# SBUF slots on multiples of 2048 bytes, and a convolution without pad columns, in a hybrid decoder layer

## Chip, cores, metric

One core of a Trainium2 chip runs the whole layer in one launch. The metric is the device time of that launch in microseconds, the median of several runs.

## What is computed

One decoder layer on T = 512 tokens with D = 1024, float32 in and out. The reference, cut to its frame:

```python
def hybrid_layer(x, ...):
    h = rms_norm(x, norm1_g)
    z = h @ w_in + b_in
    (mq, mk, mv, mo, mi, mf, fq, fk, fv, ff, rx, ry, gq, gk, gv, gg, ga, gates) = split_cols(z)
    y_ml = sigmoid(mo) * rms_norm(mlstm(mq, mk, mv, mi, mf))         # 4 heads of 128
    y_fx = forgetting_attention(fq, fk, fv, ff)                       # 4 heads of 128
    y_lru = rg_lru_branch(rx, ry, ...)     # causal conv of width 4, gates, scan, times gelu(ry)
    y_gla = silu(gg) * rms_norm(gla(gq, gk, gv, log_alpha))
    yb = einsum("bsnw,nwd->bsnd", stack([y_ml, y_fx, y_lru, y_gla]), w_branch)
    x = x + (sum over branches of sigmoid(gates) * yb) @ w_o
    h2 = rms_norm(x, norm2_g)
    return x + square(relu(h2 @ w_up)) @ w_down                       # D_FF = 4096
```

The convolution takes `y[t] = cb + cw3 x[t] + cw2 x[t-1] + cw1 x[t-2] + cw0 x[t-3]` in each channel, with x zero before the first token.

## The kernel before

**The large products.** Every product with a weight matrix is made from exact halves: a value is split into `hi` and `lo`, and hi·hi + hi·lo + lo·hi are summed in PSUM. One such product of a 128-row k-tile and 512 columns is three matmuls of 128x128 stationary and 512 moving columns, written by `Group.unit`. A group is one of two kinds. In an fm group (L266 to L268) the stationary operand is a piece of the weights (`whi`, `whi`, `wlo`) and the moving one is 512 columns of activations (`hh`, `hl`, `hh`). In a tm group (L270 to L272) the stationary operand is 128 columns of the activations (`hh`, `hh`, `hl`) and the moving one is 512 columns of the weights (`whi`, `wlo`, `whi`). There are 864 triples of the first kind and 480 of the second, 4032 matmuls. A stretch of 48 of them (4 k-tiles, 4 banks, 3 matmuls) uses one 1 MB chunk of weights; it is called a stage here.

**Weights.** 83 chunks of 1 MB come through SP's queue into `wraw` (2 buffers); ACT casts each half chunk to `whi` (L201) and DVE subtracts to get `wlo` (L202).

**Slots.** Activations live in 16 pieces of SBUF, called slots. `Slots.get` hands out the slot that has been free longest, `free` puts one back at the end. A tile's name tells both: `s7_54` is slot 7, handed out by the 54th call. A slot has 2064 float32 columns per partition, 8256 bytes, which is 32·256 + 64. In the built program the slots stand one behind the other and the weight pieces behind them; 16·8256 is 516·256. So slot i begins 64·i bytes behind slot 0 modulo 256, and `whi` and `wlo` have the residue of slot 0. The text calls the residue of a stationary piece's address minus that of a moving one, modulo 256, the **offset** of a pair; every smaller step inside a slot (512 columns, 128 columns) is a multiple of 256 bytes. With slot i against a weight piece the offset is 64·i modulo 256 where the slot is stationary, and 256 minus that where it moves: it is 0 for s0, s4, s8 and s12 alone.

**The branches.** `gens` and `pump` put pieces of the four branches (mLSTM, forgetting attention, RG-LRU, GLA) between the triples of the large products; Tile's scheduler sets each engine's final order from the program as written. `prep(n)` makes the exact halves `yhi[n]` (ACT, L442) and `ylo[n]` (DVE, L443) of a branch's result, which the projection of that branch then multiplies with `w_branch`. The convolution of the RG-LRU (L664 to L666) runs on DVE over `rx`, which holds 4 groups of 515 columns, 3 of them zero (memsets at L1141), and writes `xc`. Then come the gate products (L675, evacuated by ACT at L676 and by DVE at L677), exponentials and tanh on ACT (L686, L687), and products on DVE (L699, L700). The sigmoid of a merge gate is ACT's L883. Around the output projection, the gains of the second norm (L1171) and x are loaded again into slots, and L931 and L933 read them.

**Order.** PE, ACT, DVE and POOL each run their instructions in the order the scheduler wrote; an instruction whose data or slot is not free holds everything behind it on its engine.

Of the kernel before, what the change touches and what calls it, by code (L numbers as in the profile page):

```python
# [24 lines left out]
H = 4  # L25
# [9 lines left out]
PINC, PINK, PINN, PINS, LAG = 7, 7, 3, 4, 2  # L35
SLOT = 2064
NSLOT = 16


class Slots:  # L40
    """Eight-kilobyte pieces of SBUF, handed out and taken back in the order of emission."""

    def __init__(self, pool):
        self.pool = pool
        self.free_ids = deque(range(NSLOT))
        self.owner = {}
        self.n = 0

    def get(self, dtype=F32):
        i = self.free_ids.popleft()  # L50
        self.n += 1
        t = self.pool.tile([P, SLOT], dtype, tag=f"slot{i}", name=f"s{i}_{self.n}")
        self.owner[id(t)] = (i, t)
        return t

    def free(self, *ts):
        for t in ts:
            i, _ = self.owner.pop(id(t))
            self.free_ids.append(i)


@with_exitstack
def tile_hybrid(ctx, tc, x, norm1_g, w_in, b_in, ml_norm_g, fx_qnorm_g, fx_knorm_g, lru_conv_w,
# [38 lines left out]

    # ---------------------------------------------------------------- loads and constants
    xs = [slots.get(), slots.get()]
# [21 lines left out]
    def vector_loads():  # L126
        """Every per-channel vector as rows of 128; one transpose turns the rows into columns."""
        r = 0
# [42 lines left out]
    nc.gpsimd.memset(nhalf, -0.5)  # L171
    # selecting mask: 1 where t >= s, for [s, t]
    msel = ctile([P, P], name="msel")
    nc.gpsimd.memset(msel, 1.0)
    nc.gpsimd.affine_select(msel, msel, pattern=[[1, P]], compare_op=ALU.is_ge, fill=0.0, base=0, channel_multiplier=-1)

    # ---------------------------------------------------------------- weight stream
    # Chunks of four k-tiles by 512 columns come in whole; the exact halves hi + lo are made in pieces of two k-tiles.
    jobs, pieces = [], []
# [43 lines left out]
    def pinned(ins):  # L223
        """Keeps an instruction behind what its engine was given before it."""
        tc.keep_in_program_order(ins)
        return ins
# [23 lines left out]
    class Group:  # L250
        """One 512-column group of a product: z^T (fm) or z (tm), with a callback per finished bank."""

# [21 lines left out]
        def run(self, first=None):  # L274
            """first, where given, does the first chunk."""
            if self.pre:
# [29 lines left out]

    # ---------------------------------------------------------------- first norm, x to feature-major
    hTh = [slots.get(F32R), slots.get(F32R)]
# [8 lines left out]
    def rstd_of(ssum, n, width):  # L317
        """(ssum / n + EPS) ** -0.5 on a [128, width] tile: three Newton steps from a guess of the exponent."""
        v = tiny.tile([P, 16], F32, tag="rsv", name="rsv")[:, :width]
        y = tiny.tile([P, 16], F32, tag="rs", name="rs")[:, :width]  # L320
        t = tiny.tile([P, 16], F32, tag="rst", name="rst")[:, :width]
        nc.vector.tensor_scalar(v, ssum, 1.0 / n, EPS, op0=ALU.mult, op1=ALU.add)
        nc.vector.tensor_scalar(y.bitcast(I32), v.bitcast(I32), 1, None, op0=ALU.arith_shift_right)
        nc.vector.tensor_scalar(y.bitcast(I32), y.bitcast(I32), -1.0, float(0x5F3759DF), op0=ALU.mult, op1=ALU.add)
        for _ in range(3):
            nc.vector.tensor_mul(t, y, y)
            nc.vector.scalar_tensor_tensor(t, t, -0.5, v, op0=ALU.mult, op1=ALU.mult)
            nc.vector.scalar_tensor_tensor(y, t, 1.5, y, op0=ALU.add, op1=ALU.mult)
        return y
# [28 lines left out]

    # ---------------------------------------------------------------- small columns: ga, mi, mf, ff
    small = ctile([P, 512], name="small")  # L360
# [4 lines left out]
    def causal(ap, rows_are_queries, fill):  # L365
        """A diagonal block [128, 128]: fill where the key comes after the query."""
        sgn = 1 if rows_are_queries else -1
# [4 lines left out]
    def small_unit():  # L372
# [21 lines left out]
        yield  # L394
        # log_sigmoid of rows 64.. and its running sum over the tokens
        e = w2()
# [37 lines left out]

    # ---------------------------------------------------------------- forgetting attention
    ybr, yhi, ylo = {}, {}, {}
# [9 lines left out]
    def fox():  # L446
# [30 lines left out]
        def soft(h, tb):  # L477
            """Logits of one block of queries against the keys up to it, and their softmax."""
            n = (tb + 1) * P
# [57 lines left out]

    # ---------------------------------------------------------------- per-head norm of a token-major branch
    def norm_piece(num, tbs, hs, den=None):
        """In place: the heads hs of the blocks tbs of num [128, tb, h, 128], over their root mean square.  # L540

        With den [128, tb, h] num is first divided by it, where only the norm's EPS feels it.
        """
        nh, nt = hs.stop - hs.start, tbs.stop - tbs.start
# [18 lines left out]
    def norm_turn(num, gname, gate, y, h):  # L563
        """Head h feature-major, times its gain and gate."""
        ps = sm()
# [6 lines left out]

    # ---------------------------------------------------------------- mLSTM
    mq, mk, mv, mo = [None], [None], [None], [None]
# [56 lines left out]

    # ---------------------------------------------------------------- RG-LRU
    rx, ry = [None], [None]
    XP = 515

    def lru():
# [4 lines left out]
        lam = vecs[:, vrow["lam"] : vrow["lam"] + 4]  # L641
        # softplus(-lam) = max(-lam, 0) + log1p(exp(-|lam|)), log1p(z) = 2 atanh(z / (2 + z))
        nc.vector.scalar_tensor_tensor(z, lam, -1.0, lam, op0=ALU.mult, op1=ALU.max)
# [17 lines left out]
        for b in range(4):  # L661
            xf = rx[0][:, b * XP : (b + 1) * XP]
            s = slice(b * 512, (b + 1) * 512)
            nc.vector.tensor_scalar(xc[:, s], xf[:, 0:512], col("cw", 0 * 4 + b), col("cb", b), op0=ALU.mult, op1=ALU.add)  # L664
            for j in (1, 2, 3):
                nc.vector.scalar_tensor_tensor(xc[:, s], xf[:, j : j + 512], col("cw", j * 4 + b), xc[:, s], op0=ALU.mult, op1=ALU.add)  # L666
            yield
# [11 lines left out]
        slots.free(xc)  # L679
        # rg = 8 softplus(-lambda) r, a = exp(-rg), 1 - a^2 = tanh(rg) (1 + a^2)  # L680
        a = slots.get()
# [5 lines left out]
        nc.scalar.activation(rg[:, :2048], rg[:, :2048], AF.Tanh)  # L687
        # gelu(y) = 0.5 y (1 + tanh(sqrt(2/pi) (y + 0.044715 y^3)))
        for b in range(4):
# [31 lines left out]

    # ---------------------------------------------------------------- gated linear attention
    gqk, gv, gg = [None], [None], [None]

    def gla():
# [6 lines left out]

        # log_alpha and its sums feature-major: [128 (two heads), tokens], a pair of heads at a time
        las, ts_ = [w2(), w2()], [w2(), w2()]
# [39 lines left out]
        yield from steps(PINK)  # L774
        # k-hat token-major: [128 s, block, pair, 128]
        kh = slots.get()
# [75 lines left out]

    # ---------------------------------------------------------------- the rest of the input projection
    def ev_bias(cell, name, base=0, width=512, off=0):
# [8 lines left out]
    g_mo = fm_group(C_MO, ev_bias(mo, "mo"))  # L863
    g_rx = fm_group(C_RX, ev_bias(rx, "rx", 0, XP, 3))
    g_ry = fm_group(C_RY, ev_bias(ry, "rx", 4))
# [4 lines left out]

    # ---------------------------------------------------------------- merge groups
    merged = [None, None]
# [36 lines left out]

    # ---------------------------------------------------------------- output projection, residual  # L910
    xgh, xgl = [None, None], [None, None]
# [31 lines left out]

    # ---------------------------------------------------------------- channel mixer
    Rh, Rl = [None] * 4, [None] * 4
# [39 lines left out]

    # ---------------------------------------------------------------- order of the weight stream
    plan = [g_fq, g_fk, g_fv, g_gqk, g_gv, g_mq, g_mk, g_gg, g_mv, g_mo, g_rx, g_ry]
# [16 lines left out]

    # first chunk: the norm of each block of tokens, and the exact halves of its transpose, as the blocks come in
    sums, rstd1, pg = {}, {}, []
# [100 lines left out]

    # ---------------------------------------------------------------- run: input projection with the branches between
    g_sm = small_unit()
# [21 lines left out]
    g_gg.run()  # L1131
    mv[0] = slots.get()
    nc.gpsimd.memset(mv[0].rearrange("p (h c) -> p h c", c=129)[:, :, P : P + 1], 1.0)
    g_mv.run()
# [4 lines left out]
    rx[0] = slots.get()  # L1139
    for b in range(4):  # L1140
        nc.gpsimd.memset(rx[0][:, b * XP : b * XP + 3], 0.0)  # L1141
    g_rx.run()
# [72 lines left out]
```

## Time and profile before

| what | us |
|---|---|
| median of 3 runs | 1063.26 |
| lowest and highest run | 1063.24 and 1063.74 |
| span of the profiled execution | 1060.3 |
| PE busy in the span | 1032.8 (97%) |
| DVE, ACT, POOL busy | 489.7, 378.0, 24.4 |
| DMA, mean | 94 GB/s, 99.48 MB |

The profile gives the span of its one execution, from the first to the last instruction, and not that execution's own time; the median of the runs lies 3.0 us above the span. Busy time of PE counts a matmul from its start to its modelled end, so that neighbours overlap: the distance between the starts of two matmuls tells what one costs, and the duration in a row is longer than that. Times in the rows are from the span's start.

### The profile page before, as it was taken

How to read it: one execution, taken by the hardware profiler on the slowest of the kernel's cores; microseconds unless marked ns; L12 is line 12 of the kernel's file. 1: busy time of each engine (PE TensorE's matmuls, PEld its weight loads, DVE VectorE, ACT ScalarE, POOL GpSimd, SP SyncE). 2: the span in 40 equal slices, each digit the busy share in tenths (PEclk: the TensorE clock that was granted, in tenths of full speed). 3: DMA queues.
4: the chain of work that ended last, by engine and by line, in shares of the span. 5: the costliest groups of instructions: out<-in, count | busy, mean ns of one | idle time of the engine just before them, and what ended most of it. 6: DMA issues, size and time to landing. Idle time of an engine off the chain costs nothing.

```text
span 1060.3 us, 11180 instructions
## 1 busy us (share of the span) xinstructions
PE 1032.8 (97%) x4545; PEld 825.7 (78%) x4545; DVE 489.7 (46%) x796; ACT 378.0 (36%) x514; POOL 24.4 (2%) x66
## 2 busy tenths in 40 slices
PE   7996899999998999999999999999999999999998
PEld 5885777777877877888888888888888888888886
DVE  5583265246732887533542345554442324544221
ACT  5240444364352457332322233243431113333110
POOL 2000011000000100000000000000000000000000
PEclk9998899999999999999999999999999999999999
DMA  6569421222395212323323342223232232232321
GB/s 185 179 56 76 128 80 42 78 80 80 47 67 125 80 47 74 119 80 119 120 86 112 120 138 81 80 86 113 80 105 94 80 119 80 87 112 80 111 88 40
DMA packets 54086, 99.48 MB, mean 94 GB/s; under 512 B 7253, under 2 KB 7373, under 8 KB 54034
## 3 DMA queue, kind: packets, MB, share of 16 engines
q1 hardware_dynamic: 51762, 92.74, 32.8%
q10 hardware_dynamic: 1872, 4.72, 1.2%
q0 software_dynamic: 400, 1.31, 0.5%
q8 instruction: 35, 0.57, 0.2%
q14 instruction: 17, 0.14, 0.0%
HBM read 94.56 MB, written 2.10 MB: 91 GB/s over the span
## 4 chain that ended last, share of the span: by engine, by line
PE 91%; DMA 7%; DVE 1%; ACT 0%; SPq 0%; issue 0%; POOL 0%; DVEq 0%; ACTq 0%
PE acc L266 18%; PE acc L268 18%; PE acc L267 18%; PE acc L270 10%; PE acc L272 10%; PE acc L271 10%; DMA wraw<-in_w_in_dram 5%; DMA s<-nrows 2%; PE sm L606 1%; PE sm L481 1%; PE sm L508 1%; PE sm L675 1%; PE sm L592 0%; PE sm L498 0%; PE sm L919 0%; PE sm L467 0%
## 5 line engine op out<-in xcount | busy, mean ns | idle before, releaser
L202 DVE TENSOR_TENSOR wlo<-wraw,whi 128x1024 fp32r<-128x1024 f32 x166 | 202.6, 1223 | 386.3 <-ACT whi L201 385.1
L266 PE MATMUL acc<-s,whi 128*128 128x512 f32 x864 | 349.9, 405 | 14.3 <-DVE s L345 12.5
L268 PE MATMUL acc<-s,wlo 128*128 128x512 f32 x864 | 341.4, 395 | 0.0
L267 PE MATMUL acc<-s,whi 128*128 128x512 f32 x864 | 340.3, 394 | 0.0
L201 ACT CAST whi<-wraw 128x1024 fp32r<-128x1024 f32 x166 | 173.5, 1048 | 400.4 <-PE acc L267 183.6
L266 PEld LDWEIGHTS acc<-s,whi 128*128 128x128 f32 x864 | 163.0, 189 | 54.3 <-DVE s L345 12.7
L270 PE MATMUL acc<-whi,s 128*128 128x512 f32 x480 | 193.8, 404 | 0.2 <-ACT s L1042 0.2
L267 PEld LDWEIGHTS acc<-s,whi 128*128 128x128 f32 x864 | 163.1, 189 | 38.7 <-issue 1.9
L268 PEld LDWEIGHTS acc<-s,wlo 128*128 128x128 f32 x864 | 162.8, 188 | 38.1
L271 PE MATMUL acc<-wlo,s 128*128 128x512 f32 x480 | 190.4, 397 | 0.4 <-DVE wlo L1049 0.3
L272 PE MATMUL acc<-whi,s 128*128 128x512 f32 x480 | 190.5, 397 | 0.0
L270 PEld LDWEIGHTS acc<-whi,s 128*128 128x128 f32 x480 | 91.3, 190 | 21.9 <-ACT s L1042 0.9
L272 PEld LDWEIGHTS acc<-whi,s 128*128 128x128 f32 x480 | 90.7, 189 | 21.9 <-DVE s L1043 1.1
L271 PEld LDWEIGHTS acc<-wlo,s 128*128 128x128 f32 x480 | 90.7, 189 | 21.0 <-DVE wlo L1049 1.0
L883 ACT ACTIVATE s<-acc,vecs 128x512 f32<-128x512 f32 x32 | 22.0, 687 | 43.6 <-PE acc L268 43.6
L958 DVE TENSOR_TENSOR w<-w 128x512 f32<-128x512 f32 x32 | 22.1, 690 | 22.3 <-ACT w L956 22.3
L960 DVE TENSOR_TENSOR s<-w,s 128x512 fp32r<-128x512 f32 x32 | 22.1, 690 | 16.5 <-ACT s L959 16.5
L956 ACT ACTIVATE w<-acc 128x512 f32<-128x512 f32 x32 | 19.1, 598 | 28.7 <-PE acc L268 28.7
L959 ACT CAST s<-w 128x512 fp32r<-128x512 f32 x32 | 19.8, 619 | 25.5 <-DVE w L958 25.5
L856 ACT ACTIVATE s<-acc,vecs 128x512 f32<-128x512 f32 x28 | 18.9, 684 | 25.7 <-PE acc L268 25.6
L971 DVE SCALAR_TENSOR_TENSOR s<-acc,r,s 128x512 f32<-128x512 f32 x16 | 12.0, 749 | 31.5 <-PE acc L272 31.5
L896 DVE TENSOR_TENSOR w<-acc,s 128x512 f32<-128x512 f32 x24 | 16.4, 685 | 0.6
(212 smaller groups left out, 584.4 us busy)
## 6 DMA issues: line engine op xcount, KB each, us to landing
wraw<-in_w_in_dram SPq DMA_DIRECT2D x39, 1024.0 KB
wraw<-in_w_up_dram SPq DMA_DIRECT2D x16, 1024.0 KB
wraw<-in_w_down_dram SPq DMA_DIRECT2D x16, 1024.0 KB
wraw<-in_w_branch_dram SPq DMA_DIRECT2D x8, 1024.0 KB
wraw<-in_w_o_dram SPq DMA_DIRECT2D x4, 1024.0 KB
s<-nrows SPq DMA_DIRECT2D x8, 256.0 KB
s<-in_x_dram ACTq DMA_DIRECT2D x4, 512.0 KB
out_dram<-s ACTq DMA_DIRECT2D x8, 256.0 KB
```

The source lines that it names most:

```text
L201: nc.scalar.copy(hi, raw)
L202: nc.vector.tensor_sub(lo, raw, f32(hi))
L266: nc.tensor.matmul(ps, whi[:, k2, bs], hh, start=s0, stop=False)
L267: nc.tensor.matmul(ps, whi[:, k2, bs], hl, start=False, stop=False)
L268: nc.tensor.matmul(ps, wlo[:, k2, bs], hh, start=False, stop=s1)
L270: nc.tensor.matmul(ps, hh[:, bs], whi[:, k2], start=s0, stop=False)
L271: nc.tensor.matmul(ps, hh[:, bs], wlo[:, k2], start=False, stop=False)
L272: nc.tensor.matmul(ps, hl[:, bs], whi[:, k2], start=False, stop=s1)
L883: nc.scalar.activation(gate[0][:, b * 512 : (b + 1) * 512], ps, AF.Sigmoid, bias=col("gate", n * 8 + half * 4 + b))
L958: nc.vector.tensor_mul(t2, t, t)
L959: nc.scalar.copy(Rh[q][:, s], t2)
L960: nc.vector.tensor_sub(Rl[q][:, s], t2, f32(Rh[q][:, s]))
```

## The change

Slots 0 to 14 become 2048 floats (8192 bytes) wide, and slot 15 becomes 2560 floats wide. The wide one is given to `mv` (which needs 4·4·129 = 2064 columns), and to a call that finds the other fifteen taken. A tile of 144 columns is put among the constants, so that slot 0 begins at byte 28672 = 14·2048 of each partition; in the built program every slot, every `wraw` and every `whi` and `wlo` then begins at a multiple of 2048 bytes, and the offset of every pair is 0. Since `rx` no longer has room for pad columns, the convolution begins with tap 3 over all 512 columns and adds taps 0, 1 and 2 into 509, 510 and 511 columns; the four memsets of zeros go. Comments are removed, which moves line numbers by up to 14 (L266 to L272 become L280 to L286).

```diff
-SLOT = 2064
+SLOT = 2048
+WIDE = 2560
 NSLOT = 16
...
-        self.free_ids = deque(range(NSLOT))
+        self.free_ids = deque(range(NSLOT - 1))
+        self.wide_free = True
...
-    def get(self, dtype=F32):
-        i = self.free_ids.popleft()
+    def get(self, dtype=F32, wide=False):
+        if wide or not self.free_ids:
+            assert self.wide_free
+            self.wide_free = False
+            i = NSLOT - 1
+        else:
+            i = self.free_ids.popleft()
         self.n += 1
-        t = self.pool.tile([P, SLOT], dtype, tag=f"slot{i}", name=f"s{i}_{self.n}")
+        t = self.pool.tile([P, WIDE if i == NSLOT - 1 else SLOT], dtype, tag=f"slot{i}", name=f"s{i}_{self.n}")
...
-            self.free_ids.append(i)
+            if i == NSLOT - 1:
+                self.wide_free = True
+            else:
+                self.free_ids.append(i)
...
+    ctile([P, 144], name="pad")
     xs = [slots.get(), slots.get()]
...
         for b in range(4):
-            xf = rx[0][:, b * XP : (b + 1) * XP]
             s = slice(b * 512, (b + 1) * 512)
-            nc.vector.tensor_scalar(xc[:, s], xf[:, 0:512], col("cw", 0 * 4 + b), col("cb", b), op0=ALU.mult, op1=ALU.add)
-            for j in (1, 2, 3):
-                nc.vector.scalar_tensor_tensor(xc[:, s], xf[:, j : j + 512], col("cw", j * 4 + b), xc[:, s], op0=ALU.mult, op1=ALU.add)
+            xf, yf = rx[0][:, s], xc[:, s]
+            nc.vector.tensor_scalar(yf, xf, col("cw", 3 * 4 + b), col("cb", b), op0=ALU.mult, op1=ALU.add)
+            for j in (0, 1, 2):
+                d = 3 - j
+                nc.vector.scalar_tensor_tensor(yf[:, d:], xf[:, : 512 - d], col("cw", j * 4 + b), yf[:, d:], op0=ALU.mult, op1=ALU.add)
             yield
...
-    g_rx = fm_group(C_RX, ev_bias(rx, "rx", 0, XP, 3))
+    g_rx = fm_group(C_RX, ev_bias(rx, "rx", 0))
...
-    mv[0] = slots.get()
-    nc.gpsimd.memset(mv[0].rearrange("p (h c) -> p h c", c=129)[:, :, P : P + 1], 1.0)
+    mv[0] = slots.get(wide=True)
+    nc.gpsimd.memset(mv[0][:, : NT * H * 129].rearrange("p (h c) -> p h c", c=129)[:, :, P : P + 1], 1.0)
...
     rx[0] = slots.get()
-    for b in range(4):
-        nc.gpsimd.memset(rx[0][:, b * XP : b * XP + 3], 0.0)
     g_rx.run()
```

With fifteen slots in rotation, tiles fall on other slots. On PE, at a change of stage between 470 and 480 us, the matmuls of before read slots 4 and 6 (halves of the normed x), then 7 and 15 (halves of a branch):

```order
1718 L266 MATMUL acc3_3373<-s4_5_109,whi_3374 128x512
1719 L267 MATMUL acc3_3373<-s6_7_111,whi_3374 128x512
1720 L268 MATMUL acc3_3373<-s4_5_109,wlo_3375 128x512
1721 L266 MATMUL acc0_3498<-s7_54_3488,whi_3404 128x512
1722 L267 MATMUL acc0_3498<-s15_55_3489,whi_3404 128x512
1723 L268 MATMUL acc0_3498<-s7_54_3488,wlo_3405 128x512
```

The same place of the change, on PE:

```order
1721 L280 MATMUL acc3_3370<-s4_5_110,whi_3371 128x512
1722 L281 MATMUL acc3_3370<-s6_7_112,whi_3371 128x512
1723 L282 MATMUL acc3_3370<-s4_5_110,wlo_3372 128x512
1724 L280 MATMUL acc0_3495<-s8_54_3485,whi_3401 128x512
1725 L281 MATMUL acc0_3495<-s0_55_3486,whi_3401 128x512
1726 L282 MATMUL acc0_3495<-s8_54_3485,wlo_3402 128x512
```

The matmuls and their operands are the same; only the slots of the branch's halves are others.

The halves of the forgetting attention's result, `prep(1)`, move. On ACT before, the four casts (L442, into s10_49) stand between two evacuations of an earlier projection (L856), some twenty instructions ahead of the end of the RG-LRU (L686, L687) and of the last merge-gate evacuations (L883):

```order
220 L856 ACTIVATE s2_39_2589<-acc1_2591,vecs1_84 128x512
221 L442 CAST s10_49_3075<-s0_17_942 128x512 x4
222 L856 ACTIVATE s2_39_2589<-acc2_2592,vecs1_84 128x512
...
242 L883 ACTIVATE s7_43_2842<-acc1_2844,vecs1_84 128x512
243 L687 ACTIVATE s15_45_2947<-s15_45_2947 128x2048
244 L883 ACTIVATE s7_43_2842<-acc2_2845,vecs1_84 128x512
245 L201 CAST whi_3091<-wraw_3089 128x1024
246 L883 ACTIVATE s7_43_2842<-acc3_2846,vecs1_84 128x512
```

On ACT in the change the casts (L456) stand behind L701 (the L687 of before) and around the last L897 (L883):

```order
242 L701 ACTIVATE s0_45_2944<-s0_45_2944 128x2048
243 L897 ACTIVATE s8_43_2839<-acc2_2842,vecs2_85 128x512
244 L456 CAST s10_49_3072<-s1_17_943 128x512
245 L897 ACTIVATE s8_43_2839<-acc3_2843,vecs2_85 128x512
246 L456 CAST s10_49_3072<-s1_17_943 128x512 x3
247 L215 CAST whi_3088<-wraw_3086 128x1024
```

`yhi[1]` still gets slot 10, but slot 10 now held `xc`, which DVE's L691 (before: L677) reads last, and the cast cannot be earlier than that.

On DVE before, the four subtractions that make `ylo[1]` (L443) stand right behind that last read of `xc` and ahead of L699 and L700:

```order
440 L677 TENSOR_TENSOR s14_46_2948<-s14_46_2948,s1_44_2900 128x512
441 L443 TENSOR_TENSOR s1_50_3076<-s0_17_942,s10_49_3075 128x512 x4
442 L699 TENSOR_TENSOR w2_3053<-s8_47_3006 128x512
443 L699 TENSOR_TENSOR w2_3069<-s8_47_3006 128x512
444 L699 TENSOR_TENSOR w2_3072<-s8_47_3006 128x512
445 L699 TENSOR_TENSOR w2_3105<-s8_47_3006 128x512
446 L700 SCALAR_TENSOR_TENSOR s15_45_2947<-w2_3053,s15_45_2947 128x512
```

On DVE in the change they (L457) stand behind four L713 and three L714 (the L699 and L700 of before):

```order
451 L713 TENSOR_TENSOR w2_3102<-s11_47_3003 128x512
452 L714 SCALAR_TENSOR_TENSOR s0_45_2944<-w2_3050,s0_45_2944 128x512
453 L714 SCALAR_TENSOR_TENSOR s0_45_2944<-w2_3066,s0_45_2944 128x512
454 L714 SCALAR_TENSOR_TENSOR s0_45_2944<-w2_3069,s0_45_2944 128x512
455 L457 TENSOR_TENSOR s15_50_3073<-s1_17_943,s10_49_3072 128x512 x4
456 L714 SCALAR_TENSOR_TENSOR s0_45_2944<-w2_3102,s0_45_2944 128x512
```

`s15_50` is the wide slot, taken because the other fifteen are in use at that call. What else moves: two sets of the mLSTM's last transposes on PE stand some 24 matmuls later, and the loads of L1171 and of the second half of x, issued by ACT, now wait for slots that come free later in the last merge.

## Rows read from the trace of the kernel before

**Rows 1.** The page: busy time by engine, share of the span, instructions.

```profile
PE 1032.8 (97%) x4545; PEld 825.7 (78%) x4545; DVE 489.7 (46%) x796; ACT 378.0 (36%) x514; POOL 24.4 (2%) x66
```

**Rows 2.** The page: chain that ended last, by engine.

```profile
PE 91%; DMA 7%; DVE 1%; ACT 0%; SPq 0%; issue 0%; POOL 0%; DVEq 0%; ACTq 0%
```

**Rows 3.** Stretches: length; PE, PEld, DVE, ACT, POOL busy; clock, DMA share, GB/s.

```profile
107.00:284.00 177.00, 174.07 (x797) 136.12 (x798) 89.15 (x193) 78.83 (x130) 10.59 (x31) 0.98 0.25 77
712.00:1060.00 348.00, 344.51 (x1486) 278.56 (x1484) 125.89 (x139) 97.69 (x123) 0.00 (x0) 1.00 0.28 91
```

**Rows 4.** Waits of PE from 80 us on: us in total, times, longest.

```profile
PE acc L266 <- DVE s L345: 12.5, 1, 12.5
```

**Rows 5.** The chain in order of time, longest pieces, 70 to 420 us.

```profile
81.86 25.02 DMA wraw<-in_w_in_dram
...
284.92 21.36 DMA s<-nrows
```

**Rows 6.** Groups by line, PE, 408.00 to 1060.30 us: busy us, mean ns.

```profile
L268 PE MATMUL acc<-s,wlo 128*128 128x512 f32 x608 | 239.4, 394 | 0.0
...
L270 PE MATMUL acc<-whi,s 128*128 128x512 f32 x320 | 126.3, 395 | 0.0
```

**Rows 7.** Timeline of PE: first and last matmul of a stage on s10, s1.

```profile
441.12 0.39 PE L266 MATMUL acc<-s,whi 128*128 128x512 f32 x1
...
451.88 0.39 PE L268 MATMUL acc<-s,wlo 128*128 128x512 f32 x1
```

**Rows 8.** Timeline of PE: first and last matmul of a stage on s11, s7.

```profile
722.29 0.39 PE L266 MATMUL acc<-s,whi 128*128 128x512 f32 x1
...
733.25 0.39 PE L268 MATMUL acc<-s,wlo 128*128 128x512 f32 x1
```

**Rows 9.** Timeline of PE: first and last matmul of a stage on s0, s14.

```profile
811.39 0.39 PE L270 MATMUL acc<-whi,s 128*128 128x512 f32 x1
...
822.25 0.39 PE L272 MATMUL acc<-whi,s 128*128 128x512 f32 x1
```

**Rows 10.** Groups by line, PE, 811.35 to 822.30 us (stage on s0, s14).

```profile
L272 PE MATMUL acc<-whi,s 128*128 128x512 f32 x17 | 6.7, 397 | 0.0
L271 PE MATMUL acc<-wlo,s 128*128 128x512 f32 x16 | 6.3, 396 | 0.0
L270 PE MATMUL acc<-whi,s 128*128 128x512 f32 x16 | 6.2, 389 | 0.0
```

**Rows 11.** Groups by line, PE, 463.15 to 474.10 us (stage on s4, s6).

```profile
L268 PE MATMUL acc<-s,wlo 128*128 128x512 f32 x17 | 6.7, 395 | 0.0
L266 PE MATMUL acc<-s,whi 128*128 128x512 f32 x16 | 6.3, 393 | 0.0
```

**Rows 12.** Timeline around prep(1): ACT, then DVE, then PE.

```profile
372.08 2.17 ACT L442 CAST s<-s 128x512 fp32r<-128x512 f32 x4
...
405.42 1.91 ACT L687 ACTIVATE s<-s 128x2048 f32<-128x2048 f32 x1
407.22 0.67 ACT L883 ACTIVATE s<-acc,vecs 128x512 f32<-128x512 f32 x1
...
408.73 0.69 ACT L883 ACTIVATE s<-acc,vecs 128x512 f32<-128x512 f32 x1
...
401.11 2.50 DVE L443 TENSOR_TENSOR s<-s,s 128x512 fp32r<-128x512 f32 x4
...
407.35 1.90 DVE L700 SCALAR_TENSOR_TENSOR s<-w,s 128x512 f32<-128x512 f32 x3 [1.31 <-ACT s L687]
...
408.01 0.39 PE L267 MATMUL acc<-s,whi 128*128 128x512 f32 x1
```

**Rows 13.** The convolution, by form, DVE, 340 to 400 us.

```profile
L666 DVE SCALAR_TENSOR_TENSOR s<-s,vecs,s 128x512 f32<-128x512 f32 x12 | 8.5, 743 | 0.0
```

**Rows 14.** Timeline of DVE: last read of the gate slot, first of the gains.

```profile
653.42 0.68 DVE L896 TENSOR_TENSOR w<-acc,s 128x512 f32<-128x512 f32 x1
...
666.66 0.69 DVE L933 TENSOR_TENSOR w<-s,s 128x512 f32<-128x512 f32 x1
```

More of the change, by code (lines that the diff above doesn't have):

```diff
@@ L633, in tile_hybrid @@
     rx, ry = [None], [None]
-    XP = 515
     def lru():
```

## The prediction

> **What bounds the kernel now.** I read the page's totals first. PE is busy for 97% of the span and no other engine for half of it [rows 1]; the chain that ended last is 91% PE and 7% DMA [rows 2]. The waits of PE show one long idle stretch behind 80 us, 12.5 us in front of L266 [rows 4], and the chain names what it waited for, a weight chunk that took 25.0 us from 81.86 us on; a second stretch, from 284.92 us, is paced by a transfer of 21.4 us [rows 5]. Behind 408 us nothing holds PE: of the last 348 us it is busy for 344.5, at a granted clock of 1.00 [rows 3]. So a change is worth there what it changes in the pace of PE's matmuls, one by one.
>
> That pace is the second thing to read. 512 columns at 2.4 GHz are 213.3 ns. The last 348 us hold 1486 matmuls in 344.51 us [rows 3], 231.8 ns each, all but a few of them of 512 columns. Some 18 ns of each are not columns, about 74 us over 4032. The timeline shows that the pace is a property of a stage: from the first to the last of 48 matmuls (47 distances) it is 10.76 us on s10 and s1 [rows 7], 228.9 ns each; 10.86 us on s0 and s14 [rows 9], 231.1; 10.96 us on s11 and s7 [rows 8], 233.2. Other stages repeat these: s3/s5 and s4/s6 come many times, each time within 0.3 ns of 231, and s7/s15 twice with 233.3. What differs between stages with the same instructions is which slots they read, and a slot's number sets its offset to the weights.
>
> A row's duration moves with the distance to the next start. In the stage on s0, s14 the three lines mean (397 + 396 + 389)/3 = 394 ns [rows 10] against 231.1 of distance, so I take 163 off a duration.
>
> **What the change moves.** *Slots and weights at one residue.* Three of its matmuls are a triple, and three distances make 686.8, 693.2 and 699.6 ns in those stages. The steps between are 6.4 ns, close to 16 columns (6.67 ns); 686.7, 693.3 and 700.0 are 103, 104 and 105 times 16 columns. I read this as: a triple settles into a rhythm that is a whole number of 16-column steps, and the offsets of its three pairs choose which. With offset 0 everywhere all pairs are alike, so that one matmul must repeat by itself: 33, 34 or 35 steps, that is 220.0, 226.7 or 233.3 ns. The stage on s11, s7 shows such a rhythm already, since 11 and 7 have the same residue: offset 64 for each pair, and 233.2 ns [rows 8].
>
> Which number offset 0 gives no row of before shows outright; single pairs bound it. In the stage on s0, s14 the pairs into L270 and out of it, both with s0, have offset 0, and L270's 389 ns [rows 10] leave 226 ns. In the stage on s4, s6 the pairs into and out of L266 have offset 0, and its 393 ns [rows 11] leave 230. Both stand between pairs of other offsets, whose delays they may carry: L272 of rows 10 ends in an offset of 0 too, behind a pair of another one, and has 397. The two are nearer to 226.7 than to 233.3, and nothing is near 220, so I take 226.7 ns, and 227.0 with what is lost where small matmuls break the rhythm.
>
> Behind 408 us there are 3·608 + 3·320 = 2784 of these matmuls (the rows of the other lines have the same counts) [rows 6]. From 231.7 to 227.0 is 4.7 ns: 2784 · 4.7 = **13.1 us**. Before 408 us there are 4032 − 2784 = 1248. Up to 107 us and between 284 and 330 us DMA sets the end [rows 5], so a faster PE waits longer. The 177 and 78 us between are 255 of 408, about 780 matmuls; small matmuls of the branches stand among them (797 of all kinds in the first 177 us [rows 3]), which I let take one in six: 650 · 4.7 = 3.1 us, of which I count **2.7**, since DVE works at the side of PE from 330 to 408 us.
>
> The Trainium skill ("TensorE: Matmul & The Clock Gate", section "Back-to-back issue gap") gives N/2.4 + 2.5 ns for warm neighbours, 215.8 ns for 512 columns; this trace does not agree, its stages stand at 229 to 233 ns. If the residues alone kept this kernel from that figure, the sum by it would be 3434 · 15.9 = 55 us of gain, some 1010 us.
>
> *prep(1).* Its casts (4 in 2.17 us, 0.54 each) and subtractions (4 in 2.50 us, 0.63 each) now wait for the end of the RG-LRU [rows 12]. On ACT, L687 ends at 407.33 us and L883 of bank 2 at 407.89; the first cast ends at 408.4, L883 of bank 3 runs from 408.73 to 409.42, and three casts end at 411.0. On DVE, three L700 end at 409.25 us, then the first `ylo` ends at 409.9. PE wants it for L267 at 408.01 us [rows 12], so PE stands still for 1.9 us. The second `ylo` follows at 410.6, when PE wants it; the others have a half chunk of time. Behind the casts on ACT queue splits of weights for later stages, which lie within the 5.6 us of a half chunk. I take **2.0 us of loss**. If the cover is gone, which it is when PE arrives earlier by all it gained (2.7 us) and the RG-LRU does not, the stall is 4.7 us.
>
> *The rest.* The convolution's twelve L666 of 743 ns [rows 13] lose 1, 2 or 3 of 512 columns, 3 ns on average: nothing. The four memsets stood on POOL, which is busy for 24 us [rows 1]. The gains are now loaded behind the last read of the gate slot, which ends at 654.1 us, and are wanted at 666.66 [rows 14]: 12 us for 512 KB, which at the page's mean of 94 GB/s would take 5.6. The second half of x is issued at about the same time and wanted later. I count nothing for these; a late landing would cost its lateness, a few us at most.
>
> The sum against the profiled execution: 1060.3 of span and 3.0 around it make 1063.3, which is the median of the runs; 1063.3 − 13.1 − 2.7 + 2.0 = **1049.5 us**.
>
> **The rivals.**
>
> *A, slower: offset 0 locks at 35 steps.* Place: every large matmul. For it: the one steady stage with equal offsets has 233.2 ns [rows 8], the slowest of all stages, and nothing but single pairs speaks for 34 steps. Against it: 226 and 230 ns at offset 0 [rows 10, 11]. Price: from 231.7 to 233.3 is 1.6 ns, 3434 · 1.6 = 5.5 us and the 2.0 of prep(1): 1070.8 us. It is decided at a pace of 231.1 ns, where gain and stall are equal.
>
> *B, the residues do nothing.* The stages would differ by something that goes along with the slot. For it: DMA and the other engines run beside PE in every stage, in different measure. Against it: the same slots give the same pace again and again. The time is that of the stall alone, 1065.3 us, or 1063.3 where it is hidden. Beside it stands the Trainium skill ("SBUF — State Buffer", section "SBUF: two separate sides"), by which PE's port never waits on anyone; that rule would make this the case, and paces that go with the slots do not agree with it.
>
> *C, the stall is larger.* The pace falls as forecast, but PE waits 4.7 us at prep(1) or for the gains: 1052 to 1054 us. It needs PE to come earlier than the RG-LRU does.
>
> *D, 33 steps or fewer.* 220.0 ns would give 3434 · 11.7 = 40 us, less 2.0: 1025 us. No pair in the rows is that short.
>
> **How the numbers follow.** Forecast 0.60, A 0.17, B 0.09, C 0.10, D 0.04. The likeliest is 1049.5 us; its own range is 1043 (all 4032 matmuls count but those under DMA, 5.0 ns each, no stall: 20 us) to 1054. To hold 8 in 10 the range must take in C and B, which ends at 1065.3 and a little more for what prep(1) is uncertain by: 1043 to 1067. It leaves out A and D. Faster by over 0.2% (2.1 us; about what a measurement of this kernel tells from no change) are the forecast, C and D: 0.74. B falls half within it, 0.05, and half on its edge; with A slower is 0.21.
>
> **What will show it.** Right: behind 412 us every stage of 48 matmuls takes 47 · 226.7 = 10.65 us whatever its slots, the three lines of a kind have equal durations of about 390 ns, and PE has one new wait of about 2 us for L457 near the end of the RG-LRU. Wrong: stages of 10.97 us mean A; stages that still differ by slot mean B, and with equal pace between 226.7 and 233.3 the rule of 16 columns is wrong. A wait of PE on DVE or ACT that is longer than 3 us at prep(1), or one near the output projection, means C.

## The result, and the profile after

The changed kernel takes 1047.03 us (median of 4 runs, 1046.0 to 1052.72) against 1063.38 for the kernel before: a ratio of 0.9857, 95% interval 0.984 to 0.9874. The forecast was 1049.5 us.

The page of the changed kernel, parts 1 and 4, answers to [rows 1, 2]:

```profile
PE 1017.0 (97%) x4545; PEld 824.8 (79%) x4545; DVE 488.2 (47%) x796; ACT 377.9 (36%) x514; POOL 23.0 (2%) x62
PE 90%; DMA 7%; ACT 1%; DVE 1%; issue 0%; SPq 0%; DVEq 0%; ACTq 0%
```

PE has the same number of instructions and is busy for 15.8 us less; the span is 1045.8 us, 14.5 less. Nothing else became the bound. Groups by line of the changed kernel, PE, from 408 us to the end (busy us, mean ns), beside [rows 6]:

```profile
L282 PE MATMUL acc<-s,wlo 128*128 128x512 f32 x608 | 236.5, 389 | 0.0
L281 PE MATMUL acc<-s,whi 128*128 128x512 f32 x607 | 236.1, 389 | 0.0
L280 PE MATMUL acc<-s,whi 128*128 128x512 f32 x604 | 235.2, 389 | 0.0
L284 PE MATMUL acc<-whi,s 128*128 128x512 f32 x320 | 124.9, 390 | 0.0
```

The three lines of a stage differed by 8 ns before [rows 10], and all six lines are now at 389 to 390. The timeline of PE, first and last matmul of three stages of 48: on slots 10 and 15, on 8 and 3, and on 14 and 7:

```profile
439.34 0.39 PE L280 MATMUL acc<-s,whi 128*128 128x512 f32 x1
...
449.99 0.39 PE L282 MATMUL acc<-s,wlo 128*128 128x512 f32 x1
...
715.52 0.39 PE L280 MATMUL acc<-s,whi 128*128 128x512 f32 x1
...
726.17 0.39 PE L282 MATMUL acc<-s,wlo 128*128 128x512 f32 x1
...
802.56 0.39 PE L284 MATMUL acc<-whi,s 128*128 128x512 f32 x1
...
813.21 0.39 PE L286 MATMUL acc<-whi,s 128*128 128x512 f32 x1
```

Each takes 10.65 us for 47 distances, 226.6 ns, whatever its slots and whichever operand is stationary, against 228.9, 231.1 and 233.2 ns in [rows 7 to 9]. So do all other stages from 417.58 us on, but for four from 656.94 us on, between whose matmuls small ones (L933) stand, as before.

Waits of PE from 80 us on, changed kernel, beside [rows 4]:

```profile
PE acc L280 <- DVE s L359: 13.3, 1, 13.3
PE sm L606 <- DVE s L610: 2.8, 1, 2.8
PE acc L280 <- ACT s L870: 2.3, 1, 2.3
PE acc L280 <- ACT s L456: 0.7, 1, 0.7
...
PE acc L281 <- DVE s L457: 0.3, 1, 0.3
```

L456 and L457 are prep(1): two new waits, 1.0 us together. Its place in the timeline of the changed kernel, ACT, DVE and PE, beside [rows 12]:

```profile
402.99 1.91 ACT L701 ACTIVATE s<-s 128x2048 f32<-128x2048 f32 x1
404.79 0.68 ACT L897 ACTIVATE s<-acc,vecs 128x512 f32<-128x512 f32 x1
405.36 0.62 ACT L456 CAST s<-s 128x512 fp32r<-128x512 f32 x1
405.86 0.70 ACT L897 ACTIVATE s<-acc,vecs 128x512 f32<-128x512 f32 x1
406.45 1.66 ACT L456 CAST s<-s 128x512 fp32r<-128x512 f32 x3
...
404.93 1.90 DVE L714 SCALAR_TENSOR_TENSOR s<-w,s 128x512 f32<-128x512 f32 x3 [1.31 <-ACT s L701]
406.74 2.49 DVE L457 TENSOR_TENSOR s<-s,s 128x512 fp32r<-128x512 f32 x4
...
406.03 1.19 PE L280 MATMUL acc<-s,whi 128*128 128x512 f32 x4 [0.69 <-ACT s L456]
407.48 0.50 PE L281 MATMUL acc<-s,whi 128*128 128x512 f32 x1 [0.26 <-DVE s L457]
```

The RG-LRU ends as much earlier as PE comes (L701 at 404.9, L687 of before at 407.33), and the scheduler put four L280, which need the casts alone, ahead of the first L281, which needs a subtraction. So PE has something to do while DVE finishes.

Where, in the two profiled executions, the 14.4 us between the starts of the last large matmul (1056.12 and 1041.69 us) lie, by matmuls counted from the first: 1.4 us are gained by the 861st (279.86 and 278.46 us), 1.2 more by the 1241st (405.92 and 403.36 us), 1.2 are lost again over the 56 behind it, at prep(1), and 13.1 us are gained from there to the end.

### The profile page after: what moved, and what is told of

Read it like the earlier page. It is cut to its first block, busy times and chain, and to the rows that moved or that the text cites. A ratio compares the mean times of both kernels' runs of the same rounds, so it can differ in the third digit from the quotient of the medians.

```text
span 1045.8 us, 11175 instructions
## 1 busy us (share of the span) xinstructions
PE 1017.0 (97%) x4545; PEld 824.8 (79%) x4545; DVE 488.2 (47%) x796; ACT 377.9 (36%) x514; POOL 23.0 (2%) x62
## 4 chain that ended last, share of the span: by engine, by line
PE 90%; DMA 7%; ACT 1%; DVE 1%; issue 0%; SPq 0%; DVEq 0%; ACTq 0%
PE acc L281 17%; PE acc L282 17%; PE acc L280 17%; PE acc L284 10%; PE acc L286 10%; PE acc L285 10%; DMA wraw<-in_w_in_dram 4%; DMA s<-nrows 2%; PE sm L620 1%; PE sm L495 1%; PE sm L522 1%; PE sm L689 1%; DMA s<-in_x_dram 1%; PE sm L606 1%; PE sm L512 0%; PE sm L933 0%
## 5 line engine op out<-in xcount | busy, mean ns | idle before, releaser
L280 PE MATMUL acc<-s,whi 128*128 128x512 f32 x864 | 346.8, 402 | 16.2 <-DVE s L359 13.3
L281 PE MATMUL acc<-s,whi 128*128 128x512 f32 x864 | 337.7, 391 | 0.3 <-DVE s L457 0.3
L280 PEld LDWEIGHTS acc<-s,whi 128*128 128x128 f32 x864 | 163.0, 189 | 53.0 <-DVE s L359 13.5
L284 PE MATMUL acc<-whi,s 128*128 128x512 f32 x480 | 192.1, 400 | 0.6 <-ACT s L1056 0.5
L281 PEld LDWEIGHTS acc<-s,whi 128*128 128x128 f32 x864 | 163.2, 189 | 35.5 <-issue 1.9
L285 PE MATMUL acc<-wlo,s 128*128 128x512 f32 x480 | 188.2, 392 | 0.4 <-DVE wlo L1063 0.4
L286 PE MATMUL acc<-whi,s 128*128 128x512 f32 x480 | 188.3, 392 | 0.0
L286 PEld LDWEIGHTS acc<-whi,s 128*128 128x128 f32 x480 | 90.5, 189 | 20.1 <-DVE s L1057 1.2
L897 ACT ACTIVATE s<-acc,vecs 128x512 f32<-128x512 f32 x32 | 22.0, 686 | 42.4 <-PE acc L282 42.4
```

The lines of the kernel that those rows point to most:

```text
L280: nc.tensor.matmul(ps, whi[:, k2, bs], hh, start=s0, stop=False)
L281: nc.tensor.matmul(ps, whi[:, k2, bs], hl, start=False, stop=False)
L284: nc.tensor.matmul(ps, hh[:, bs], whi[:, k2], start=s0, stop=False)
L285: nc.tensor.matmul(ps, hh[:, bs], wlo[:, k2], start=False, stop=False)
L286: nc.tensor.matmul(ps, hl[:, bs], whi[:, k2], start=False, stop=s1)
L897: nc.scalar.activation(gate[0][:, b * 512 : (b + 1) * 512], ps, AF.Sigmoid, bias=col("gate", n * 8 + half * 4 + b))
```

## The experiments

**Only the pitch.** The kernel before, with all addresses at one residue and nothing else changed: convolution, pads, sixteen slots in one queue and the order of every engine stay.

```diff
-SLOT = 2064
+SLOT = 2048
+WIDE = 2112
...
-        t = self.pool.tile([P, SLOT], dtype, tag=f"slot{i}", name=f"s{i}_{self.n}")
+        t = self.pool.tile([P, WIDE if i in (10, 15) else SLOT], dtype, tag=f"slot{i}", name=f"s{i}_{self.n}")
...
```

> The kernel before with slots of 2048 columns, but slots 10 and 15 (those of rx and mv) of 2112: every slot and weight piece has the same residue modulo 256, which is 192, and none is at a multiple of 2048. Convolution, pads, the sixteen slots and the order of every engine are those of before. Theory (the offset alone makes the gain): every stage behind 408 us runs at 226.7 ns, 13 us less there, 1.7 to 2.7 us less ahead of it, and no stall at prep(1), so 1045 to 1049 us. Rival (multiples of 2048, or the convolution or the other rotation of slots, make the gain): 1062 to 1064 us.

Measured 1046.08 us, a ratio of 0.983 (0.9812 to 0.9847). Groups by line of this kernel, PE, 715 to 1041 us:

```profile
L272 PE MATMUL acc<-wlo,s 128*128 128x512 f32 x256 | 99.7, 389 | 0.0
L267 PE MATMUL acc<-s,whi 128*128 128x512 f32 x223 | 86.8, 389 | 0.0
```

The whole gain comes with the residue alone. Slots and weights begin at 192 modulo 256 here, so multiples of 2048 are not needed. No wait for prep(1) is among those of PE.

**Only the convolution.** The kernel before with the convolution of the change (as in the diff of the change), no pads, no memsets, and slots of 2064.

> The kernel before with the convolution of the change (509 to 511 columns, no pads, no memsets) and the slots of before. Theory: no effect, 1062.5 to 1064.5 us, stages at 229 to 233 ns as before. Rival (the convolution is part of the gain): 1061 us or less.

Measured 1063.85 us, a ratio of 1.000 (0.9991 to 1.001). The convolution does nothing by itself; it makes room for slots of 2048.

**All weights 64 bytes further.**

```diff
-WIDE = 2560
+WIDE = 2576
```

> The changed kernel with the wide slot 16 columns wider (2576), which puts all weight pieces 64 bytes further: offset 64 in fm groups, 192 in tm groups, all slots and the order as in the change. Theory (offset decides, and equal pairs lock): fm stages at 233.3 ns as the stage on s11, s7 of before; tm stages at one number of 220.0, 226.7 or 233.3. With 233.3 in both, 6.6 ns on some 3430 matmuls that pace the end is 22.7 us: 1070 us; with tm at 226.7, about 1062. Rival (equal residues of the slots among themselves are enough): 1047 us.

Measured 1067.34 us, a ratio of 1.0036 (1.0025 to 1.0046): the gain is gone and a little more, with every slot still on a multiple of 2048. Groups by line, PE: an fm stretch (712 to 780 us), then two tm stages (805.1 to 816.2 and 1006.1 to 1017.0 us):

```profile
L280 PE MATMUL acc<-s,whi 128*128 128x512 f32 x98 | 38.7, 394 | 0.0
...
L286 PE MATMUL acc<-whi,s 128*128 128x512 f32 x17 | 6.8, 398 | 0.0
...
L286 PE MATMUL acc<-whi,s 128*128 128x512 f32 x17 | 6.6, 389 | 0.0
L285 PE MATMUL acc<-wlo,s 128*128 128x512 f32 x16 | 6.3, 395 | 0.0
L284 PE MATMUL acc<-whi,s 128*128 128x512 f32 x16 | 6.3, 392 | 0.0
```

At offset 64 the fm stages run at 233.3 ns, as forecast. At offset 192 the tm stages show two rhythms, 233.3 ns in the first half of the down projection (8 stages) and 229.0 in the second (8 stages), with the same offsets: the offset alone does not decide there.

**All weights 128 bytes further** (WIDE = 2592).

> The changed kernel with the wide slot 32 columns wider (2592): all weight pieces 128 bytes further, offset 128 in both kinds of group. Theory (as the blocks of matmuls alone: 233.4 ns at 128): 233 ns in fm and tm stages, 6.7 ns on 3430 matmuls, 1069 to 1072 us. Rival (the kernel's triples find a shorter rhythm than the blocks): 229 to 231 ns and 1055 to 1063 us.

One run, 1066.78 us, below the expected times. The distances behind 408 us average 232.8 (fm) and 233.2 ns (tm), so the pace is the expected one. From the 1241st matmul to the last this kernel takes 16.8 us longer than the change, and 2.4 us lie ahead of it. The expectation had counted 18.7 and 4.4 us there (6.7 ns on 2784 and on some 650 matmuls).

**Offsets by themselves.** This kernel leaves out the layer. A line for each offset, here offset 64 (16 columns of 4 bytes):

```python
for i in range(n): nc.tensor.matmul(banks[i // 12 % 4], sta[:, i % 2 * 256 + 16 : i % 2 * 256 + 144], mov[:, i % 3 * 512 : i % 3 * 512 + 512], start=i % 12 == 0, stop=i % 12 == 11)
```

> This kernel leaves out the layer: it loads x, makes one moving and one stationary tile of it and runs blocks of 48 matmuls (128x128 stationary, 512 moving columns, each into one of four PSUM banks), a block for each offset between the stationary and the moving address, 0 to 240 bytes in steps of 16, then other steps, float32r and after that bfloat16; its output is not that of the layer. All tiles begin at a residue of 128 modulo 256, none at a multiple of 2048. Theory (only the offset modulo 256 counts): offset 0 gives 226.7 ns from start to start, and 256, 384 or 512 give the same; offset 64 gives 233.3; the others lie at 220.0, 226.7 or 233.3, whole numbers of 16 columns. Rival (the address itself must be a multiple of 2048): no block gives 226.7, offset 0 neither. Rival (nothing but the offset's stage neighbours): all blocks alike.

Timeline of PE: the first matmul of the block at offset 0 (L44) and of the next block, then the same at 64 (L48) and for bfloat16 (L75); 48 distances lie between the two of a pair.

```profile
33.39 0.39 PE L44 MATMUL bank<-mov,sta 128*128 128x512 f32 x1
...
44.27 0.39 PE L45 MATMUL bank<-mov,sta 128*128 128x512 f32 x1
...
77.55 0.39 PE L48 MATMUL bank<-mov,sta 128*128 128x512 f32 x1
...
88.75 0.39 PE L49 MATMUL bank<-mov,sta 128*128 128x512 f32 x1
...
377.42 0.39 PE L75 MATMUL bank<-movb,stab 128*128 128x512 bf16 x1
...
387.79 0.38 PE L76 MATMUL bank<-movb,stab 128*128 128x512 bf16 x1
```

10.88 us are 226.7 ns, 11.20 are 233.3, 10.37 are 216.0. In the last 24 distances of each block, offsets 256, 512 and 768 gave 226.7 ns like 0 (384, which the expectation names with them by mistake, is 128 modulo 256 and gave 232.1); of the offsets between, 16 and 240 gave 226.7 too and all other multiples of 16 gave 228.9 to 234.4, several of them (230.0, 231.8, 234.4) no whole number of sixteen-column steps, neither for one matmul nor for three. Eight offsets in bfloat16 all gave 215.8 ns. The first rival falls too: tiles at a residue of 128 reach 226.7.

**Other shapes.** Blocks as above, the layer left out.

> This kernel leaves out the layer too: blocks of 48 matmuls of other shapes at offsets 0, 64, 128 and 192 (128, 64 and 32 stationary columns, 512, 384 and 256 moving ones, float32r), two blocks in bfloat16, two in plain float32, and offsets in steps of 4 bytes around 0. Theory L (the reads of the weight load delay the stream of the running matmul): fewer stationary columns, less excess over the columns' own time, about half of 13 to 20 ns at 64; fewer moving columns, the same excess for each matmul. Rival M (each moving column costs more by the offset): the excess falls with the moving columns, half at 256, and stays with 64 stationary ones. Offsets up to 16 bytes either side of 0 give 226.7 only where they are multiples of 16.

Groups by line, PE: float32r at offset 0 with 512 (L48), 384 (L52) and 256 (L56) moving columns, the same at offset 64 (L49, L53, L57), at offset 0 with 64 (L60) and 32 (L64) stationary columns, and with 64 stationary and 256 moving ones (L68); plain float32 at offsets 0 (L74) and 128 (L75):

```profile
L74 PE MATMUL bank<-movf,staf 128*128 128x512 f32 x96 | 41.5, 593 | 0.0
L75 PE MATMUL bank<-movf,staf 128*128 128x512 f32 x96 | 41.4, 592 | 0.0
...
L49 PE MATMUL bank<-mov,sta 128*128 128x512 f32 x48 | 11.4, 395 | 0.0
...
L64 PE MATMUL bank<-mov,sta 128*32 128x512 f32 x48 | 11.3, 394 | 0.0
...
L60 PE MATMUL bank<-mov,sta 128*64 128x512 f32 x48 | 11.2, 392 | 0.0
...
L48 PE MATMUL bank<-mov,sta 128*128 128x512 f32 x48 | 11.0, 389 | 0.0
...
L53 PE MATMUL bank<-mov,sta 128*128 128x384 f32 x48 | 8.6, 338 | 0.0
...
L52 PE MATMUL bank<-mov,sta 128*128 128x384 f32 x48 | 8.5, 335 | 0.0
...
L56 PE MATMUL bank<-mov,sta 128*128 128x256 f32 x48 | 5.9, 283 | 0.0
...
L57 PE MATMUL bank<-mov,sta 128*128 128x256 f32 x48 | 5.8, 281 | 0.0
...
L68 PE MATMUL bank<-mov,sta 128*64 128x256 f32 x48 | 5.6, 276 | 0.0
```

Neither theory holds throughout. In the last 24 distances of each block, 512, 384 and 256 moving columns take 226.7, 173.3 and 120.0 ns at offset 0; that is 13.3 ns over the columns' own time each, as theory L says. At offset 64 they take 233.3, 176.7 and 117.8 ns, an excess of 20.0, 16.7 and 11.1, nearly what rival M says. So with 256 moving columns offset 0 is the slowest of the four offsets (117.8 to 118.8 ns at the others). Fewer stationary columns do not lower the excess with 512 moving ones (230.0 ns with 64 and 231.7 with 32, at offset 0), but 64 halve it with 256 (113.3 ns against 120.0). The last expectation fell too: offset 16, at 226.7 ns in the blocks above, ran at 233.3 here behind other blocks, 240 at 228.3, and offset 252 at 226.7. Offset 0 gave 226.7 in every block of both kernels that had 128 stationary columns and 512 moving ones.

**All triples.** Blocks as above, with pairs a, a, b.

> This kernel leaves out the layer: blocks of 36 matmuls (128x128 stationary, 512 moving columns, float32r) in triples whose three pairs have the offsets a, a, b, as a triple of the layer has, with a and b from 0 to 240 bytes in steps of 16: 256 blocks. Theory (a triple's rhythm is a whole number of 16-column steps, 102 at offset 0): the means of the blocks lie at 226.7, 228.9, 231.1 and 233.3 ns, 0, 0 gives 226.7, and none is lower. Rival (offset 0 is only one of several good layouts): some a, b with 224.4 ns or less, which would be worth 2784 times 2.2 ns = 6 us or more behind 408 us.

The mean distance in ns (last 24 of 36) for b = 0, 16, ..., 240, at a = 0, 16, 64, 128, 192 and 240:

```
a=0    226.7 226.7 233.3 232.2 231.1 231.0 232.6 233.3 231.1 226.7 233.3 231.1 231.1 231.1 231.1 226.7
a=16   226.7 226.7 233.3 233.3 231.1 233.3 234.0 233.3 228.9 233.3 233.3 232.2 233.3 233.1 233.5 232.5
a=64   233.3 233.3 231.1 233.3 233.3 228.9 231.1 235.5 231.1 235.5 232.2 233.3 231.8 231.1 233.3 233.1
a=128  233.3 232.2 233.3 231.1 230.0 231.1 233.3 231.1 232.8 232.6 233.3 233.9 233.1 230.0 232.2 232.0
a=192  228.9 229.7 228.9 231.1 228.9 231.1 228.9 233.3 233.5 232.2 233.3 232.2 228.9 234.5 233.3 228.9
a=240  233.3 226.7 232.2 234.5 227.8 229.5 230.6 233.4 229.9 226.7 232.2 230.6 228.4 230.4 232.2 226.7
```

None of the 256 is below 226.7, and eight besides 0, 0 reach it. The rival falls: no other layout of these operands found here beats one residue for all. That the means lie at four values alone fell as well.

**The old rotation of slots.** The change with sixteen slots in one queue, as before; slot 15 stays the wide one.

```diff
-        self.free_ids = deque(range(NSLOT - 1))
+        self.free_ids = deque(range(NSLOT))
```

> The change without its new way of handing out slots: all sixteen slots in one queue as before (mv falls on slot 15 by itself, which is the wide one), layout on multiples of 2048 and convolution as in the change. Theory (prep(1) costs the change what its trace shows, 1.3 to 1.6 us): 1 to 1.6 us faster than the changed kernel in the same job, some 1045.5 us against 1046.8. Rival (what is lost at prep(1) is given back later, since nothing else is on the path): the same within 0.1%.

> The changed kernel itself, beside the run with the old rotation on the same chip. All theories: 1046 to 1048 us. It tells the size of the difference between the two.

Measured 1047.15 us (1045.21 to 1048.27; ratio 0.9841, 0.9826 to 0.9855) against 1049.11 for the change measured beside it (1045.85 to 1050.8; 0.9866, 0.985 to 0.9883). The medians lie 2.0 us apart the expected way, and the intervals overlap: inconclusive by time. Nor is that difference the one of prep(1): of the two profiled executions the one with the old rotation is the slower (1048.27 against 1045.85 us) and starts the 1241st large matmul, ahead of prep(1), 4.0 us later, at 405.66 against 401.69 us. The traces tell more from there on. Timeline of PE, the 1241st and the 1297th large matmul, of the change first and then of the kernel with only the pitch:

```profile
403.36 0.39 PE L281 MATMUL acc<-s,whi 128*128 128x512 f32 x1
...
417.58 0.39 PE L280 MATMUL acc<-s,whi 128*128 128x512 f32 x1
```

```profile
403.66 0.39 PE L268 MATMUL acc<-s,whi 128*128 128x512 f32 x1
...
416.36 0.39 PE L267 MATMUL acc<-s,whi 128*128 128x512 f32 x1
```

The same 56 matmuls take 14.22 us with the new rotation and 12.70 with the old one (12.69 in the run with the old rotation above, 14.24 in the repeat of the change). The new hand-out costs 1.5 us here, and behind it the change and the kernel with only the pitch run alike: 593.51 us each for the 2600 matmuls from the 1401st on. So the fastest version here is the layout without the new rotation, by 1.5 us in the traces; a difference as small as that was not separated by time.

## Why the prediction was right

**The pace** was read rightly: stages differ by the slots that they read, that is an address, and one residue for all takes 226.7 ns. Behind prep(1) the trace has 13.1 us, as the sum had for all behind 408 us.

**The reading of why 226.7** was too strict. It said that with equal pairs one matmul must repeat by itself, so that only 220.0, 226.7 and 233.3 are possible. Offset 192 gave 229.0 in eight stages with the three lines at 392, 395 and 389 ns, and 233.3 in eight others. What holds is less: at 128 stationary and 512 moving columns offset 0 came to 226.7 after every stage and every interruption, and some other offsets have more than one rhythm; that what ran before picks one of them is likely, and no run tests it. The prediction also paired each stationary piece with the moving operand of the matmul ahead of it; no run tells that from the matmul's own moving operand, since in every kernel here one of the two kinds of operand has a single residue throughout. The choice of 34 steps over 35 rested on single pairs and could have gone wrong; that such pairs stood at 226 and 230 ns pointed the right way, and rival A's 233.3 is the number of offset 64, where it was measured again.

**Ahead of 408 us** the sum had 2.7, and the two profiled executions differ by 2.56 at the 1241st matmul. That these agree is luck. What the pace gave is steady from trace to trace, and it is less: from the 385th to the 861st matmul the four kept traces with one residue (the change, its repeat, the pitch alone, the old rotation) take 144.4 us and the four with other offsets 145.7 to 145.9, so 1.2 us are gained; from the 1057th to the 1241st the change gains 0.2 us (58.88 and 58.65 us). Most of the rest came between the 861st and the 1057th matmul, where DMA sets part of the pace and the eight traces take 65.4 to 69.2 us. Two stretches of before, then the same two of the change; the third number from the end is the granted clock:

```profile
284.30:330.70 46.40, 40.49 (x178) 31.24 (x176) 16.45 (x32) 22.72 (x30) 3.09 (x8) 1.00 0.88 91
330.70:407.80 77.10, 77.08 (x361) 61.05 (x362) 58.59 (x131) 40.72 (x58) 3.21 (x8) 0.98 0.21 69
```

```profile
283.00:330.00 47.00, 41.50 (x177) 32.30 (x175) 16.34 (x32) 22.56 (x30) 3.08 (x8) 0.96 0.86 90
330.00:406.00 76.00, 75.28 (x360) 59.62 (x360) 55.34 (x128) 39.40 (x55) 3.21 (x8) 1.00 0.22 70
```

A piece of half clock of 3.4 us, behind a wait of PE for data, lay at 332 us before, where PE set the pace, and at 308 us in the change, where a transfer did. Eight matmuls at 0.2 us more each, 1.6 us, are covered by that transfer. The prediction had no term for this. Its place goes with the residue: 331.5 to 332.1 us in all four traces with other offsets, 307.0 to 309.9 us in all four with one residue; what moves it was not found. The old rotation's trace has a second such piece, of 6.8 us from 329.0 us on, which makes it the later one of the two profiled executions above.

**prep(1)** is mis-sized as well: 2.0 us forecast, 1.5 measured against the pitch alone. The sum put all of it on `ylo`; the traces have 0.85 us at the first cast (2.67 us from the 1241st to the 1249th matmul, against 1.82) and 0.68 in the 16 matmuls behind it (4.30 against 3.62). The step that made PE stand still for L267's `ylo` overlooked the four L280 that the new order puts ahead of it; and PE did not come earlier than the RG-LRU, so rival C did not come about.

**The rest** was nothing, as said: the convolution measured none, and the gains, whose slot's last read ends at 648.4 us, are used at 660.58 without a wait.

**The basis** was off too. 1047.54 us of the profiled execution over a span of 1045.8 leave 1.7 us around the span, not 3.0, and 17 further executions of the kernel before leave 1.6 to 1.8. So its profiled execution took some 1062.0 us (an estimate from these), 1.3 below the median from which the sum was made. This 1.3, the 0.5 of prep(1) and the 0.5 by which the profiled execution of the change lies above its median are most of the 2.5 us between forecast and result.

**Rival B** falls with the run of the pitch alone. The two rules cited can be placed now. The Trainium skill ("TensorE: Matmul & The Clock Gate", section "Back-to-back issue gap") gives 215.8 ns for 512 columns as the gap of an isolated matmul; the bfloat16 blocks agree with 215.8, and float32r does not, with 226.7 at best. For a stream the same section gives about 131 ns, with which no run here agrees: 215.8 is the shortest at 512 columns. The Trainium skill's rule that PE's port never waits on anyone ("SBUF — State Buffer", section "SBUF: two separate sides") is about contention between engines; in agreement with it, offset 0 gives 226.7 ns in blocks with every other engine idle as in the layer beside DVE and ACT. The offset between PE's own two operands does set its pace here.

## What to carry over

Where a kernel is a stream of float32r matmuls of 128 stationary and 512 moving columns, compare the distance between starts from stage to stage. If it goes with the buffers that are read, lay stationary and moving operands out at one residue modulo 256; a pitch that is a multiple of 256 bytes keeps it, and nothing larger is needed. For other shapes measure first: with 256 moving columns offset 0 was the slowest of four. Change the pitch alone: a new rotation of buffers that comes along moves dependences, and here gave 1.5 us back. Take the time around the span from an execution that has both.

## What the runs showed of the hardware

- A float32r matmul of 128 stationary and 512 moving columns (213.3 ns of columns at 2.4 GHz) follows the one ahead after 226.7 to 235.5 ns, by the offset between stationary and moving operand. bfloat16 gives 215.8 ns at all eight offsets run, and plain float32 429.2 ns for each of the two records of a matmul at the two offsets run.
- The excess over the columns' own time depends on offset and shape together: 13.3 ns at offset 0 with 512, 384 and 256 moving columns, but 20.0, 16.7 and 11.1 at offset 64; 64 stationary columns give 16.7 ns with 512 moving ones and 6.7 with 256, at offset 0.
- Some offsets other than 0 have two steady rhythms (229.0 and 233.3 ns at 192; 226.7 and 233.3 at 16). What in PE makes them was not found: the runs tell offsets, columns and types apart, not what the weight load and the stream share.
